# A decoder trunk on one core: high weight parts cast apart from low ones at the mixer's end, and a later place for two transposes

## The chip, the cores and the metric

The kernel runs on one core of one Trainium2 chip. The metric is device time in microseconds (us) of one execution, as the median of several runs. Five engines work side by side, each through its own list of instructions in a fixed order: PE (TensorE: matmuls and transposes), DVE (VectorE), ACT (ScalarE), POOL (GpSimd) and SP, which here only issues the copies of weights from memory (DMAs).

## The reference

The model takes 256 tokens of 1024 channels through two layers. Each layer is: half a gated FFN, a mixer, half a gated FFN, each on a normalised input and added to the residual.

```
for layer in range(2):
    h = rms_norm(x, ffn1_norm[layer])
    x = x + 0.5 * swiglu(h, gate, up, down)          # d_ff = 2816
    h = rms_norm(x, mix_norm[layer])
    if layer == 0:                                   # "mixer AB"
        proj = h @ ab_w_in                           # 1024 -> 1536
        u_pool, u_val, u_gate = split(proj)          # 512 each
        y_pool = pool_mixer(u_pool)                  # 4 windows, a 128x128 map each, a scale
        y_conv = conv_module(u_val, u_gate)          # GLU, 31 taps, LayerNorm, swish
        y = concat(y_pool, y_conv) @ ab_w_out
    else:                                            # "mixer C", sparse attention
        y = dsa_attention(...) @ c_w_out
    x = x + y
    h = rms_norm(x, ffn2_norm[layer])
    x = x + 0.5 * swiglu(h, gate, up, down)
return rms_norm(x, final_norm)
```

## The kernel before

All weights are float32 in memory. Each weight tile is split on the chip into a high part `hi` (a cast, on ACT, line 158) and a low part `lo` = raw - hi (on DVE, line 182), and a product is made of three: hi x hi, lo x hi and hi x lo. The activations are split in the same way (`hT` holds the normalised input, transposed, high and low; `kh`/`kl` are the high and low parts of a hidden tile).

Weight tiles come in one fixed `stream` and are of two kinds: `gu` (1024 input channels by 256 columns, 1 MB, cast and subtracted in two pieces) and `d` (128 rows by 1024 columns, 0.5 MB, one piece). There are three raw buffers of each kind; a raw buffer is free for the next copy when the tile's low part is made (`issue`, line 130). There are three high and three low buffers of `gu`, five of `d`. `pump(n)` makes the high and the low part of the next n tiles that have buffers, the two always together; `weights(kind)` pumps until the tile that is needed is split.

The stages are written out by hand in program order, and every engine works in that order: there is no scheduler that moves anything. The 256 tokens are two halves of 128, token tile A and token tile B. At the end of each stage `tail` (line 352) does the last four K tiles of the output product for tile A, in two column halves with accumulators `a0`, `a1`, then for tile B (`b0`, `b1`). Behind each half, `norm_half` adds the sum to the residual `x` (DVE, line 227) and squares it (ACT, line 229); `norm_apply` makes the reciprocal root (POOL, line 235) and the two scaled halves `h` (DVE, line 238). A's two halves are transposed on PE (line 245) between the K tiles of `b1`, and copied to `hT` as high (ACT, line 249) and low (DVE, line 252). B's two halves are transposed by `finish_b`, in the middle of the next stage's first matmuls.

The next stage begins in `wide` (line 292): three `gu` tiles, numbered 0, 1, 2 below. The first pass (line 304) takes A's tokens with the high parts of tiles 0 and 1, then come B's transposes, then the pass of tile 2. The second pass goes tile by tile: B's tokens with the high part (line 312), all tokens with the low part (line 315), two column halves each. From the fourth tile on the FFN goes on with `hidden` (lines 284 and 287) and `down_all` (line 341).

I call the stretch from the last K tiles of one stage to the second pass of the next a seam. The seam that the change touches is the one from mixer AB (`mixer_ab`) to the second FFN. There, before, the call of `tail` has `units` (0, 0), so nothing is pumped behind a half, and `between` 1, so one tile is pumped between the residual sums of A's first and second half: it is tile 0 of the FFN. Tiles 1 and 2 are pumped when `wide` is called. In the middle of mixer AB, `pool_map` maps two pooled groups: two matmuls into two halves of one PSUM bank, then for each half a scaled cast on ACT (line 598) and the rest on DVE (line 599).

Of the kernel before, what the change touches and what calls it, by code (L numbers as in the profile page):

```python
# [39 lines left out]
def tile_trunk(ctx: ExitStack, tc: tile.TileContext, d: dict, out: bass.AP):  # L40
# [35 lines left out]
    def f32(ap):  # L76
        return ap.bitcast(F32)
# [106 lines left out]
            issue()  # L184
        return True

    def weights(kind):
        k = state["used"]
        state["used"] += 1
        assert stream[k][0] == kind, (k, stream[k], kind)  # L190
        while order[kind].index(k) >= split[kind]:
            assert pump(1), ("no buffer", k, kind)
        return parts[k]

    def done(kind, n=1):
        spent[kind] += n
# [95 lines left out]
    def wide(items, finish_b, pumps=True, ahead=2):  # L292

        banks = []
        for n, (w, cols, _) in enumerate(items):
            if n == len(items) - 1:
                finish_b()
            bs = []
            for cs, tag in cols:
                m = cs.stop - cs.start  # L300
                b = bank(tag)
                bv = b[:m].rearrange("p (l n) -> p l n", l=2)
                for c in range(NCH):
                    pe.matmul(bv[:, :, 0:P], w[0][:, c, cs], hT[:, c, 0:2, 0:P],  # L304
                              start=c == 0, stop=False, skip_group_check=True)
                bs.append((bv, cs))
            banks.append(bs)
        pump(ahead)
        for (w, cols, use), bs in zip(items, banks):
            for bv, cs in bs:  # L310
                for c in range(NCH):
                    pe.matmul(bv[:, :, P:2 * P], w[0][:, c, cs], hT[:, c, 0:2, P:2 * P],  # L312
                              start=False, stop=False, skip_group_check=True)
                for c in range(NCH):
                    pe.matmul(bv[:, 0, :], w[1][:, c, cs], hT[:, c, 0, :],  # L315
                              start=False, stop=c == NCH - 1, skip_group_check=True)
            done("gu")
            use([bv for bv, _ in bs])
            if pumps:
                pump(1)  # L320
# [28 lines left out]
    def new_accs():  # L349
        return [[bank(ATAG[t][h]) for h in range(2)] for t in range(2)]  # L350

    def tail(accs, kts, ws, coef, g, units=(1, 1), between=0):

        n = len(kts)

        def mm(t, half, k):
            down_mm(accs[t][half], kts[k], ws[k], t, half, False, k == n - 1)

        ss = small(2)
        for half in range(2):  # L360
            for k in range(n):
                mm(0, half, k)
            pump(units[half])
            norm_half(0, half, accs[0], coef, ss)
            if half == 0:
                pump(between)
        ha = list(norm_apply(0, ss, g))
        for k in range(n):
            mm(1, 0, k)
        for k in range(n):  # L370
            mm(1, 1, k)
            if k < 2:
                transpose_half(0, k, ha, ATAG[0][k])
        done("d", n)
        ss = small(2)
        for half in range(2):
            norm_half(1, half, accs[1], coef, ss)
        hb = list(norm_apply(1, ss, g))

        def finish_b():  # L380
            for half in range(2):
                transpose_half(1, half, hb, ATAG[1][half])
        return finish_b
# [12 lines left out]
    def ffn(n, finish_b, gname, final=None, extra=None, first=None):  # L396
# [20 lines left out]
        else:  # L417
            tags = [("g0", "g1"), ("g2", "g3"), ("a0", "a1")]
            two = (slice(0, P), slice(P, 2 * P))
            wide([(weights("gu"), list(zip(two, tags[i])), use(i)) for i in range(3)], finish_b)  # L420
        g = load_gain(gname)
        accs = None
        for i in range(3, NFF):
# [74 lines left out]
    def mixer_ab(finish_b, gname):  # L498
# [90 lines left out]
        def pool_map(first, tag):  # L589
            b = bank(tag)  # L590
            outs = [b[:, q * 256:q * 256 + 256] for q in range(2)]
            for q, o in enumerate(outs):
                gi = first + q
                pe.matmul(o, pw[:, gi * P:gi * P + P], ms[gi], start=True, stop=True)
            for q, o in enumerate(outs):
                gi = first + q
                hi, lo = new_split()
                act.activation(hi, o, AF.Copy, scale=pscale[:, gi:gi + 1])
                dve.scalar_tensor_tensor(lo, o, pscale[:, gi:gi + 1], f32(hi),
                                         op0=ALU.mult, op1=ALU.subtract)  # L600
                kts.append((hi, lo))

        accs = {}
        ws = []
# [91 lines left out]
        tags = [("a0", "a1"), ("g0", "g1"), ("g2", "g3")]  # L696
        two = (slice(0, P), slice(P, 2 * P))
        preload(AF.Sigmoid)
        wide([(weights("gu"), list(zip(two, t)), use) for t in tags], finish_b, True, AHEAD)
        taps_pe(0, "b0")  # L700
        taps_out(0)
        load_pack(2)
# [12 lines left out]
        taps_out(3)  # L715
        preload(AF.Silu)
        last = weights("gu")
        b01 = bank("g0")
        p01 = b01[:, 0:256], b01[:, 256:512]
        narrow_group(p01[0], last, slice(0, P))  # L720
# [5 lines left out]
        out_mm(0, 0)  # L726
        out_mm(1, 0)
        windows(0, p01)
        variance("g2")
        out_mm(0, 1)  # L730
        pool_diff(0)
# [10 lines left out]
        out_mm(0, 3)  # L742
        out_mm(1, 3)
        accs = [accs[0], accs[1]]
        return tail(accs, kts[4:8], [weights("d") for _ in range(4)], 1.0, g, (0, 0), 1)


    def bias_rows(tag):
# [15 lines left out]
    def mixer_c(finish_b, gname):  # L764
# [11 lines left out]
        def use_kw(bvs):  # L776
            wide_sum(bvs[0], 72, kw)
            pool.dma_start(k2[64:128], kw[0:64])

        two = (slice(0, P), slice(P, 2 * P))  # L780
        wide([(weights("gu"), list(zip(two, ("g0", "g1"))), use_qi(0)),
              (weights("gu"), list(zip(two, ("g2", "g3"))), use_qi(1)),
              (weights("gu"), [(slice(0, 72), "a0")], use_kw)], finish_b)
        g = load_gain(gname)


# [376 lines left out]
```

## Time and profile before

| | |
|---|---|
| median of 3 runs | 988.77 us (988.34 to 989.34) |
| profiled execution, its own time | 987.02 us |
| its span in the profile | 985.3 us |
| PE busy | 963.4 us, 98% of the span |
| DVE busy | 658.6 us, 67% |
| ACT busy | 534.3 us, 54% |
| share of the chain that ended last | PE 92%, DVE 4%, ACT 2%, issue 2% |
| mean granted clock of PE | 0.993 of 2.4 GHz |

The span is what the profiler sees of the program; 1.7 us of the execution's own time lie around it. The chain that ended last is followed back from the last instruction, at each step to what released it. PE carries nearly all of it, so what can be saved here is the time in which PE waits or runs at its lower clock.

### The profile page before, as it was taken

The page shows a single profiled execution, that of the slowest core. Times are in us where ns is not written, and L with a number is a line of the kernel's source. Part 1 is how long each engine was busy: PE and PEld are TensorE (multiplying, and loading weights), DVE is VectorE, ACT ScalarE, POOL GpSimd, SP SyncE. Part 2 cuts the span into 40 slices and gives each one's busy share as a digit, 9 for nine tenths or more (in the row PEclk, how much of TensorE's full clock was granted, in tenths as well). Part 3 has the DMA queues.
Part 4 walks back from the last instruction along what each step waited for, and adds up shares of the span by engine and source line. Part 5 has one row for each costly group of instructions (what it writes and reads, how often), then busy time and mean ns, then how long its engine had stood idle before and what let it go on. Part 6 is the DMA issues. An engine that isn't in the chain of part 4 may idle for free.

```text
span 985.3 us, 14682 instructions
## 1 busy us (share of the span) xinstructions
PE 963.4 (98%) x5720; PEld 836.3 (85%) x5720; DVE 658.6 (67%) x1083; ACT 534.3 (54%) x959; POOL 62.3 (6%) x89
## 2 busy tenths in 40 slices
PE   7999999999979999999999999999999999999997
PEld 6888888898869888888988888888899798888885
DVE  6876666678568666666686666667888658666653
ACT  5665555565556645554565555445556556555542
POOL 3000000000000000000000000000435000000000
PEclk9999999999999999999999999999999999999999
DMA  9875555535246757655365555437444527655401
GB/s 335 305 278 186 191 190 188 187 109 181 65 148 230 264 205 244 237 194 190 111 254 192 192 192 193 162 107 279 148 137 151 210 71 253 232 189 191 155 1 43
DMA packets 38021, 182.03 MB, mean 185 GB/s; under 512 B 6416, under 2 KB 6448, under 8 KB 24768
## 3 DMA queue, kind: packets, MB, share of 16 engines
q1 hardware_dynamic: 32400, 169.92, 48.6%
q0 software_dynamic: 5264, 10.92, 3.4%
q8 instruction: 45, 0.74, 0.3%
q10 hardware_dynamic: 288, 0.27, 0.1%
q14 instruction: 24, 0.20, 0.1%
HBM read 179.92 MB, written 4.22 MB: 187 GB/s over the span
## 4 chain that ended last, share of the span: by engine, by line
PE 92%; DVE 4%; ACT 2%; issue 2%; DMA 0%; POOL 0%; SPq 0%; POOLq 0%; DVEq 0%; ACTq 0%
PE g L284 29%; PE g L287 15%; PE a L341 14%; PE b L341 13%; PE g L268 4%; PE g L312 2%; PE g L315 2%; PE g L304 2%; PE a L268 1%; DVE lo L182 1%; PE b L538 1%; PE a L312 1%; PE a L315 1%; PE b L823 1%; DVE keep L969 1%
## 5 line engine op out<-in xcount | busy, mean ns | idle before, releaser
L182 DVE TENSOR_TENSOR lo<-raw,hi 128x1024 fp32r<-128x1024 f32 (+1 forms) x319 | 380.4, 1244 | 57.8 <-ACT hi L158 57.8
L158 ACT CAST hi<-raw 128x1024 fp32r<-128x1024 f32 x320 | 314.7, 1043 | 5.4 <-DMA raw<-in_c_out 2.6
L284 PE MATMUL g<-hT,hi 128*128 128x512 f32 x1248 | 310.7, 391 | 0.8 <-DVE t L327 0.8
L284 PEld LDWEIGHTS g<-hT,hi 128*128 128x128 f32 x1248 | 228.7, 188 | 44.8 <-DVE t L327 1.0
L324 ACT COPY t<-g 128x256 f32<-128x256 f32 x174 | 63.4, 372 | 222.2 <-PE g L287 205.9
L287 PEld LDWEIGHTS g<-hT,lo 128*128 128x128 f32 x1248 | 170.3, 190 | 12.2
L287 PE MATMUL g<-hT,lo 128*128 128x256 f32 x1248 | 174.0, 282 | 0.0
L327 DVE TENSOR_TENSOR t<-g,t 128x256 f32<-128x256 f32 x174 | 71.9, 421 | 137.2 <-ACT t L324 137.0
L341 PE MATMUL a<-hi,kh 128*128 128x512 f32 x208 | 82.7, 398 | 0.0
L341 PE MATMUL b<-hi,kh 128*128 128x512 f32 x208 | 82.6, 397 | 0.0
L341 PE MATMUL a<-lo,kh 128*128 128x512 f32 x208 | 81.9, 394 | 0.0
L341 PE MATMUL b<-hi,kl 128*128 128x512 f32 x208 | 81.5, 392 | 0.0
L341 PE MATMUL b<-lo,kh 128*128 128x512 f32 x208 | 81.5, 392 | 0.0
L341 PE MATMUL a<-hi,kl 128*128 128x512 f32 x208 | 81.0, 389 | 0.0
L392 ACT CAST kh<-t 128x256 fp32r<-128x256 f32 x88 | 35.7, 406 | 57.8 <-DVE t L390 57.8
L393 DVE TENSOR_TENSOR kl<-t,kh 128x256 fp32r<-128x256 f32 x88 | 37.4, 425 | 41.5 <-ACT kh L392 41.5
L388 ACT ACTIVATE t<-t 128x256 f32<-128x256 f32 x88 | 36.9, 420 | 26.1 <-DVE t L327 26.1
L235 POOL TENSOR_TENSOR sm<-sm,mhalf 128x1 f32<-128x1 f32 x11 | 6.1, 554 | 673.2 <-DVE sm L233 673.2
L341 PEld LDWEIGHTS a<-hi,kl 128*128 128x128 f32 x208 | 39.1, 188 | 8.8
L341 PEld LDWEIGHTS b<-hi,kl 128*128 128x128 f32 x208 | 39.3, 189 | 8.3
L341 PEld LDWEIGHTS b<-hi,kh 128*128 128x128 f32 x208 | 39.4, 189 | 8.2
L341 PEld LDWEIGHTS b<-lo,kh 128*128 128x128 f32 x208 | 39.4, 189 | 7.8
(210 smaller groups left out, 949.9 us busy)
## 6 DMA issues: line engine op xcount, KB each, us to landing
raw<-in_gu SPq DMA_DIRECT2D x87, 1024.0 KB, 4.8
raw<-in_dn SPq DMA_DIRECT2D x88, 512.0 KB, 5.3
raw<-in_c_qk SPq DMA_DIRECT2D x8, 1024.0 KB, 4.9
raw<-in_ab_in SPq DMA_DIRECT2D x6, 1024.0 KB, 4.8
raw<-in_ab_out SPq DMA_DIRECT2D x8, 512.0 KB, 5.2
raw<-in_c_v SPq DMA_DIRECT2D x8, 512.0 KB, 4.3
raw<-in_c_out SPq DMA_DIRECT2D x8, 512.0 KB, 4.0
eall<-escr POOLq DMA_DIRECT2D x4, 768.0 KB, 17.3
```

Source lines behind the costliest of these rows:

```text
L158: act.copy(hi[:, c], raws[k][:, c])
L182: e.tensor_tensor(lo[:, c], raws[k][:, c], f32(hi[:, c]), op=ALU.subtract)
L268: pe.matmul(dst, wt[:, c, cols], hT[:, c, part, :], start=n == 0, stop=n == len(seq) - 1)
L284: pe.matmul(b, hi[:, c, cols], hT[:, c, 0:2, :], start=c == 0, stop=False, skip_group_check=True)
L287: pe.matmul(b[:, 0:256], lo[:, c, cols], hT[:, c, 0, :], start=False, stop=c == NCH - 1, skip_group_check=True)
L312: pe.matmul(bv[:, :, P:2 * P], w[0][:, c, cs], hT[:, c, 0:2, P:2 * P], start=False, stop=False, skip_group_check=True)
L324: act.copy(t[:m], bv[:, 1, :])
L327: dve.tensor_tensor(dst[:m], bv[:, 0, :], t[:m], op=ALU.add)
L341: pe.matmul(acc, kt[a][:, ts], w[b][:, hs], start=start and n == 0, stop=stop and n == 2)
L388: act.activation(s, gv, AF.Silu)
L392: act.copy(hi, m)
L393: dve.tensor_tensor(lo, m, f32(hi), op=ALU.subtract)
```

## The change

Three things change, and all of them move instructions in mixer AB and in the seam behind it.

1. The high parts of `gu` tiles can be cast apart from the low parts. In mixer AB, behind its last input tile, tile 0 of the next FFN is pumped whole and the high part of tile 1 is cast; behind the pooled windows, the high part of tile 2. `wide` takes tiles whose high parts are there (`ahead_of`), and its `pump(ahead)` makes the low parts of tiles 1 and 2 behind B's transposes. No tile is pumped any more between the residual sums of A's halves. In the other seams `ahead_of` finds all tiles split, and the order of instructions is the same as before.
2. `pool_map` casts both groups on ACT first, then takes both rests on DVE.
3. In this seam A's transposes stand behind the second and the third K tile of `b1` instead of the first and the second.

```
+    def highs(n):
+        for _ in range(n):
+            assert begun["gu"] - spent["gu"] < hi_bufs["gu"]
+            begin("gu")
+
+    def ahead_of(kind):
+        k = take(kind)
+        while order[kind].index(k) >= begun[kind]:
+            highs(1)
+        return k
...
+    def lows(kind, k):
         while order[kind].index(k) >= split[kind]:
             assert pump(1), ("no buffer", k, kind)
...
         pump(ahead)
-        for (w, cols, use), bs in zip(items, banks):
+        for (k, cols, use), bs in zip(items, banks):
+            lows("gu", k)
+            w = parts[k]
...
-    def tail(accs, kts, ws, coef, g, units=(1, 1), between=0):
+    def tail(accs, kts, ws, coef, g, units=(1, 1), turn=(0, 1)):
...
             norm_half(0, half, accs[0], coef, ss)
-            if half == 0:
-                pump(between)
...
             mm(1, 1, k)
-            if k < 2:
-                transpose_half(0, k, ha, ATAG[0][k])
+            if k in turn:
+                transpose_half(0, turn.index(k), ha, ATAG[0][turn.index(k)])
...
+            new = [new_split() for _ in outs]
             for q, o in enumerate(outs):
-                gi = first + q
-                hi, lo = new_split()
-                act.activation(hi, o, AF.Copy, scale=pscale[:, gi:gi + 1])
-                dve.scalar_tensor_tensor(lo, o, pscale[:, gi:gi + 1], f32(hi),
-                                         op0=ALU.mult, op1=ALU.subtract)
-                kts.append((hi, lo))
+                act.activation(new[q][0], o, AF.Copy, scale=pscale[:, first + q:first + q + 1])
+            for q, o in enumerate(outs):
+                dve.scalar_tensor_tensor(new[q][1], o, pscale[:, first + q:first + q + 1],
+                                         f32(new[q][0]), op0=ALU.mult, op1=ALU.subtract)
+            kts.extend(new)
...
         last = weights("gu")
+        pump(1)
+        highs(1)
         b01 = bank("g0")
...
         windows(0, p01)
+        highs(1)
         variance("g2")
...
-        return tail(accs, kts[4:8], [weights("d") for _ in range(4)], 1.0, g, (0, 0), 1)
+        return tail(accs, kts[4:8], [weights("d") for _ in range(4)], 1.0, g, (0, 0), (1, 2))
```

The first place is DVE in the seam, from A's first residual sum (`x_86`) and second (`x_87`) to its scaled halves `h`. Before:

```order
L227 SCALAR_TENSOR_TENSOR x_86<-a_463_2625,x_86 128x512
L182 TENSOR_TENSOR lo_2805<-raw_2106,hi_2802 128x1024 x2
L227 SCALAR_TENSOR_TENSOR x_87<-a_464_2626,x_87 128x512
L233 SCALAR_TENSOR_TENSOR sm_2825<-sm_2786 128x1
L238 SCALAR_TENSOR_TENSOR h_2829<-x_86,sm_2827,gain_2508 128x512
L238 SCALAR_TENSOR_TENSOR h_2831<-x_87,sm_2827,gain_2508 128x512
```

And now:

```order
L247 SCALAR_TENSOR_TENSOR x_86<-a_467_2636,x_86 128x512
L247 SCALAR_TENSOR_TENSOR x_87<-a_468_2637,x_87 128x512
L253 SCALAR_TENSOR_TENSOR sm_2831<-sm_2800 128x1
L258 SCALAR_TENSOR_TENSOR h_2835<-x_86,sm_2833,gain_2508 128x512
L258 SCALAR_TENSOR_TENSOR h_2837<-x_87,sm_2833,gain_2508 128x512
```

The two pieces of tile 0's low part (`lo_2805`) are gone from between the sums; on ACT the two casts of its high part are gone from between the squares.

The second place is DVE a little later, from the sums of tile B (`x_88`, `x_89`) to the low part of B's transposes (`hT` from `b`). Before:

```order
L227 SCALAR_TENSOR_TENSOR x_89<-b_466_2634,x_89 128x512
L233 SCALAR_TENSOR_TENSOR sm_2878<-sm_2871 128x1
L238 SCALAR_TENSOR_TENSOR h_2882<-x_88,sm_2880,gain_2508 128x512
L238 SCALAR_TENSOR_TENSOR h_2884<-x_89,sm_2880,gain_2508 128x512
L182 TENSOR_TENSOR lo_2889<-raw_2173,hi_2886 128x1024 x2
L182 TENSOR_TENSOR lo_2897<-raw_2239,hi_2894 128x1024 x2
L252 TENSOR_TENSOR hT<-b_539_2938,hT 128x4x128
L252 TENSOR_TENSOR hT<-b_540_2945,hT 128x4x128
```

And now:

```order
L247 SCALAR_TENSOR_TENSOR x_89<-b_470_2645,x_89 128x512
L253 SCALAR_TENSOR_TENSOR sm_2884<-sm_2877 128x1
L258 SCALAR_TENSOR_TENSOR h_2888<-x_88,sm_2886,gain_2508 128x512
L258 SCALAR_TENSOR_TENSOR h_2890<-x_89,sm_2886,gain_2508 128x512
L272 TENSOR_TENSOR hT<-b_535_2928,hT 128x4x128
L272 TENSOR_TENSOR hT<-b_536_2935,hT 128x4x128
L182 TENSOR_TENSOR lo_2960<-raw_2173,hi_2556 128x1024 x2
L182 TENSOR_TENSOR lo_2965<-raw_2239,hi_2664 128x1024 x2
```

The low parts of tiles 1 and 2 moved from ahead of `hT`'s low part to behind it; on ACT the four casts of their high parts are gone from ahead of `hT`'s high part, to the middle of the mixer.

The third place is PE in the same seam: the matmuls of `b1` (three for each K tile) and the transposes of A's halves (`ident`). Before:

```order
L341 MATMUL b_466_2634<-hi_2387,kl_2706 128x512
L245 MATMUL a_520_2848<-ident,h_2829 128x128 x4
L341 MATMUL b_466_2634<-hi_2676,kh_2710 128x512
L341 MATMUL b_466_2634<-lo_2678,kh_2710 128x512
L341 MATMUL b_466_2634<-hi_2676,kl_2711 128x512
L245 MATMUL a_521_2858<-ident,h_2831 128x128 x4
```

And now:

```order
L364 MATMUL b_470_2645<-hi_2387,kl_2720 128x512
L364 MATMUL b_470_2645<-hi_2690,kh_2724 128x512
L364 MATMUL b_470_2645<-lo_2692,kh_2724 128x512
L364 MATMUL b_470_2645<-hi_2690,kl_2725 128x512
L265 MATMUL a_522_2857<-ident,h_2835 128x128 x4
L364 MATMUL b_470_2645<-hi_2744,kh_2729 128x512
L364 MATMUL b_470_2645<-lo_2746,kh_2729 128x512
L364 MATMUL b_470_2645<-hi_2744,kl_2730 128x512
L265 MATMUL a_523_2867<-ident,h_2837 128x128 x4
```

Each group of four transposes stands three matmuls further on.

## Rows read from the trace of the kernel before

**Rows 1.** Timeline of PE at the mixer seam: start, duration (us), instruction, count, [idle before <- releaser].

```profile
269.59 0.39 PE L341 MATMUL b<-hi,kh 128*128 128x512 f32 x1
...
277.18 0.66 PE L245 MATMUL a<-ident,h 128*128 128x128 f32 x4 [4.03 <-DVE h L238]
...
281.78 2.06 PE L304 MATMUL g<-hT,hi 128*128 128x256 f32 x16
...
291.02 1.33 PE L312 MATMUL g<-hT,hi 128*128 128x256 f32 x8 [1.11 <-DVE hT L252]
```

**Rows 2.** Timeline of PE at the seam from the second FFN to the third.

```profile
464.08 0.39 PE L341 MATMUL b<-hi,kh 128*128 128x512 f32 x1
...
467.49 0.60 PE L245 MATMUL a<-ident,h 128*128 128x128 f32 x4
...
468.62 0.60 PE L245 MATMUL a<-ident,h 128*128 128x128 f32 x4
...
470.45 4.00 PE L304 MATMUL g<-hT,hi 128*128 128x256 f32 x32
474.29 1.30 PE L245 MATMUL b<-ident,h 128*128 128x128 f32 x8
475.34 2.15 PE L304 MATMUL a<-hT,hi 128*128 128x256 f32 x16
477.33 1.12 PE L312 MATMUL g<-hT,hi 128*128 128x256 f32 x8
```

**Rows 3.** PE's waits, whole span: engine line <- releaser, us in total, times, longest.

```profile
PE g L312 <- DVE hT L252: 1.1, 1, 1.1
PE g L304 <- ACT hi L158: 0.8, 2, 0.6
```

**Rows 4.** Two windows: engines' busy time (count), then PE's granted clock, DMA share, GB/s.

```profile
279.00:280.00 1.00, 1.00 (x6) 0.90 (x5) 0.18 (x1) 0.20 (x1) 0.00 (x0) 0.50 0.00 0
283.00:284.00 1.00, 0.84 (x8) 0.64 (x6) 0.16 (x1) 1.00 (x3) 0.17 (x1) 1.00 0.00 0
```

**Rows 5.** Timeline of DVE at the mixer seam.

```profile
269.32 0.69 DVE L227 SCALAR_TENSOR_TENSOR x<-a,x 128x512 f32<-128x512 f32 x1
271.74 2.36 DVE L182 TENSOR_TENSOR lo<-raw,hi 128x1024 fp32r<-128x1024 f32 x2 [1.73 <-ACT hi L158]
274.01 0.68 DVE L227 SCALAR_TENSOR_TENSOR x<-a,x 128x512 f32<-128x512 f32 x1
...
285.74 4.63 DVE L182 TENSOR_TENSOR lo<-raw,hi 128x1024 fp32r<-128x1024 f32 x4
```

**Rows 6.** Timeline of DVE at the seam from the second FFN to the third.

```profile
469.88 0.69 DVE L252 TENSOR_TENSOR hT<-a,hT 128x512 fp32r<-128x512 f32 x1 [0.44 <-ACT hT L249]
470.49 1.28 DVE L227 SCALAR_TENSOR_TENSOR x<-b,x 128x512 f32<-128x512 f32 x2
...
473.46 1.42 DVE L238 SCALAR_TENSOR_TENSOR h<-x,sm,gain 128x512 f32<-128x512 f32 x2 [0.67 <-POOL sm L235]
475.58 1.35 DVE L252 TENSOR_TENSOR hT<-b,hT 128x512 fp32r<-128x512 f32 x2 [0.71 <-ACT hT L249]
```

**Rows 7.** Timeline of ACT in the middle of the mixer.

```profile
247.92 0.47 ACT L598 ACTIVATE kh<-g,cpk 128x256 fp32r<-128x256 f32 x1 [7.55 <-PE g L594]
248.94 0.48 ACT L598 ACTIVATE kh<-g,cpk 128x256 fp32r<-128x256 f32 x1 [0.55 <-DVE kl L599]
...
253.96 1.05 ACT L158 CAST hi<-raw 128x1024 fp32r<-128x1024 f32 x1 [0.74 <-PE b L341]
```

**Rows 8.** Timeline of DVE in the middle of the mixer.

```profile
248.43 0.48 DVE L599 SCALAR_TENSOR_TENSOR kl<-g,cpk,kh 128x256 fp32r<-128x256 f32 x1 [2.31 <-ACT kh L598]
249.45 0.48 DVE L599 SCALAR_TENSOR_TENSOR kl<-g,cpk,kh 128x256 fp32r<-128x256 f32 x1 [0.55 <-ACT kh L598]
```

**Rows 9.** Timeline of SP's issues, and the raw weights' time from issue to landing.

```profile
218.16 15.93 SPq L145 DMA_DIRECT2D raw<-in_gu  x3
...
DMA to landing us min/median/max: 3.4/4.9/7.3
```

More of the change, by code (lines that the diff above doesn't have):

```diff
@@ L185, in pump, with take @@
         return True
-    def weights(kind):
+    def highs(n):
+        for _ in range(n):
+            assert begun["gu"] - spent["gu"] < hi_bufs["gu"]
+            begin("gu")
+    def take(kind):
         k = state["used"]
@@ L190, in weights @@
         assert stream[k][0] == kind, (k, stream[k], kind)
+        return k
[3 more added lines that the diff above has]
+            highs(1)
+        return k
+    def weights(kind):
+        k = take(kind)
+        lows(kind, k)
+        return parts[k]
+    def lows(kind, k):
         while order[kind].index(k) >= split[kind]:
             assert pump(1), ("no buffer", k, kind)
-        return parts[k]
     def done(kind, n=1):
@@ L298, in wide @@
             bs = []
+            w = parts[w]
             for cs, tag in cols:
@@ L419, in ffn @@
             two = (slice(0, P), slice(P, 2 * P))
-            wide([(weights("gu"), list(zip(two, tags[i])), use(i)) for i in range(3)], finish_b)
+            wide([(ahead_of("gu"), list(zip(two, tags[i])), use(i)) for i in range(3)], finish_b)
         g = load_gain(gname)
@@ L698, in mixer_ab @@
         preload(AF.Sigmoid)
-        wide([(weights("gu"), list(zip(two, t)), use) for t in tags], finish_b, True, AHEAD)
+        wide([(ahead_of("gu"), list(zip(two, t)), use) for t in tags], finish_b, True, AHEAD)
         taps_pe(0, "b0")
@@ L780, in mixer_c @@
         two = (slice(0, P), slice(P, 2 * P))
-        wide([(weights("gu"), list(zip(two, ("g0", "g1"))), use_qi(0)),
-              (weights("gu"), list(zip(two, ("g2", "g3"))), use_qi(1)),
-              (weights("gu"), [(slice(0, 72), "a0")], use_kw)], finish_b)
+        wide([(ahead_of("gu"), list(zip(two, ("g0", "g1"))), use_qi(0)),
+              (ahead_of("gu"), list(zip(two, ("g2", "g3"))), use_qi(1)),
+              (ahead_of("gu"), [(slice(0, 72), "a0")], use_kw)], finish_b)
         g = load_gain(gname)
```

## The prediction

> **What bounds the kernel now.** The page gives PE 98% of the span and nearly all of the chain that ended last, so I read the profile from PE. PE's list of waits comes first: the two waits of [rows 3], together 1.9 us, lie at the mixer seam, as does a single wait of 4.03 us for A's scaled halves [rows 1]. Then the timelines of the mixer seam [rows 1] and of the seam from the second FFN to the third [rows 2], which has the same instructions in the same order on PE and none of these waits. The reader should lay one over the other, from the first matmul of `b0` to the first matmul of the second pass (L312): 291.02 - 269.59 = 21.43 us at the mixer, 477.33 - 464.08 = 13.25 us at the FFN seam. The excess, 8.18 us, is what this seam can give.
>
> Where it lies: in the FFN seam fifteen matmuls stand between 464.08 and the transposes at 467.49, so one takes 0.2273 us. At the mixer PE is through with the same fifteen at 272.99 and the transposes begin at 277.18: 4.19 us late. From there to the first pass takes 281.78 - 277.18 = 4.60 us against 470.45 - 467.49 = 2.96: 1.64 us. The window of 279 to 280 shows why, a granted clock of 0.50, which is the lower level, 1.2 GHz; it follows PE's 4.03 us without work, and at 283 to 284 it is 1.00 again [rows 4]. Then 0.8 us of waiting for casts of high parts and 1.1 for the low part of `hT` [rows 3]. That makes 7.7; the other 0.45 I put down to the restarts.
>
> DVE shows the cause [rows 5]. A's first residual sum starts at 269.32, its second only at 274.01; between them stands tile 0's low part (2.36 us), which itself waited 1.73 us for ACT's casts. At 285.74 four more pieces (4.63 us) stand ahead of B's `hT`.
>
> **A's chain.** With no tile between the halves, the second sum follows the first at 269.32 + 0.70 = 270.02; the last matmul of `a1` is issued by then, since `b0` starts at 269.59. From second sum to first transpose took 277.18 - 274.01 = 3.17 us, so the first half could be transposed at 273.19. PE is through the first K tile of `b1` at 272.99 and through the second 3 x 0.2273 = 0.68 us later, at 273.67, which is where the transposes now stand. So PE doesn't wait for A at all, the 4.19 us go, and the lower clock with them.
>
> **B's chain, and what the later place costs.** I count from the first matmul of `b0`, at 0. A's transposes begin after 18 matmuls, at 4.09; those of the second half 468.62 - 467.49 = 1.13 later, at 5.22; the end of `b1` stays at 470.45 - 464.08 = 6.37. DVE takes A's low parts ahead of B's sums. In the FFN seam the second low part starts 469.88 - 468.62 = 1.26 behind its transposes, B's sums 0.61 after that, B's two `h` 2.97 after those and last 1.42 [rows 6]. Here: low part 6.48, sums 7.09, `h` 10.06 to 11.48. PE's first pass, 3.84 long in the FFN seam (470.45 to 474.29), ends at about 10.2 to 10.6, the upper end if it waits for A's second low part (7.17 at the end). So PE now waits for `h`: the second half's four transposes start at 11.5 and end 0.53 later (half of 475.34 - 474.29), at 12.03; the pass of tile 2 takes 477.33 - 475.34 = 1.99, so L312 starts at 14.02, say 14.05 with one handover. The FFN seam has 13.25: the later place of the transposes costs 0.8 us. If DVE got to B's sums sooner than I count, it costs nothing; more than 0.8 it can't well cost, since everything moves by one K tile, 0.68, and small waits. B's `hT` low part ends 475.58 + 1.35 - 475.34 = 1.59 behind the transposes, at 13.6, ahead of L312.
>
> **The moved casts and low parts.** Ahead of `pool_map` come four cast pieces on ACT, at 1.05 each 4.2 us [rows 7], and two low pieces on DVE, 2.36 us [rows 5]. ACT had been idle for 7.55 us there [rows 7], DVE for 2.31 [rows 8]. On ACT 3.3 us of cover are left. On DVE the low part overruns its cover by 0.05 us, but the rest now waits for both casts anyway. The raw data must be there: the third of the copies left SP at 218.16 + 15.93 - 0.33 = 233.8 and the slowest landing took 7.3 us, so all had landed by 241.1 [rows 9], when ACT has just begun. The last two pieces (tile 2) stand ahead of the cast at 253.96, which had waited 0.74 us; it moves by about 1.3 us, its low part is taken when DVE gets to it, and PE wants it only in the tail. I take nothing for all this; with no cover it would be at most the 4.2 us of ACT. On SP the copy of the fourth tile moves ahead of three copies of `d` tiles, and starts when tile 0's raw buffer comes free, some 25 us sooner than before. It delays nothing, for those `d` copies wait for their own buffers.
>
> Behind B's `hT` DVE has tiles 1 and 2 to do, 2.36 each: done at 13.6 + 2.4 = 16.0 and 18.3. PE wants the first at 14.05 + 4.8 = 18.9 (two column halves of 1.92, then 0.96 of high parts; L312 and L315 take 0.96 each in the FFN seam), the second at 22.7: 2.9 and 4.4 us of cover. The sums that follow them in the queue, and the low parts of tiles 3 and 4, come up to 5 us later than now against the second pass. PE needs tile 3 only 11.5 us after L312 begins, and a DVE that is 67% busy makes up 5 us in two or three tiles.
>
> **`pool_map`.** ACT's second cast waited 0.55 us for DVE, though DVE was reading the other half of the bank [rows 7, 8]: the engines took turns, 247.92 to 249.93 for one map. Now two casts, then two rests: one handover instead of three, and two like instructions overlap by about 0.1 (B's two sums take 1.28, one takes 0.69). Some 0.25 a map, two maps. DVE is ahead of PE by little there, so I take 0.15 us for the start of `b0`; the bounds are 0 and 0.5.
>
> **The sum.** L312 moves from 291.02 to 269.59 - 0.15 + 14.05 = 283.49, 7.5 us sooner. Behind it PE is busy with matmuls to the next seam, so nothing eats the gain. Span 985.3 - 7.5 = 977.8, the execution's own time 987.02 - 7.5 = 979.5. The profiled execution is 1.75 us below the median of the three runs, so the median is 988.77 - 7.5 = **981.3 us**. About 0.2%, 2 us, is what a measurement of this kernel can tell from no change.
>
> **The rivals.** (1) The later place costs nothing, because DVE takes B's sums sooner than I count: the seam then has the FFN's 13.25, and the gain is 8.18 + 0.15 = 8.3, so 980.5. For it: with the earlier place PE would wait only 0.2 us, so both places are near each other. Against: DVE's fixed order. Chance 0.17.
>
> (2) A new wait. The low parts of tiles 1 and 2 come late, at L315 of tile 1. It decides when they are over 2.9 us later than I count, as when B's `hT` is itself late by casts still ahead of it; then B's chain keeps its old waits and only A's goes: 4.19 + 1.64 - 0.8 = 5.0 us, 983.8. Against: both orders show nothing ahead of `hT`. Chance 0.07.
>
> (3) The clock drops all the same, in the three short waits of up to 0.9 us in sum that the seam keeps, and costs the 1.64 us again: 982.9. Against: at 283 to 284 the clock was 1.00 while PE waited 0.6 us for a cast [rows 3, 4]. Chance 0.04. The Trainium skill has this rule in "TensorE: Matmul & The Clock Gate", section "A second HAM failure mode: psum-queue depth-cycling": small idle gaps between groups of matmuls can make the clock swing between its two levels. By that rule the sum would be rival 3's; the trace so far disagrees for waits of this size.
>
> (4) Slower. ACT is held at the cast of tile 1's high part, ahead of `pool_map`, because its high buffer or its raw data isn't free; everything behind it in the mixer, and PE with it, waits. Each us past 247.9 counts in full, and it outweighs the gain from 7.5 us on, when the cast ends past 255.4. 4 us more than that would give 993. Against: landing by 241.1, and three high buffers for one tile in use. Chance 0.03.
>
> (5) No change that can be told: the seam's gain is given back in the FFN, where DVE starts with 5 us of arrears. It needs PE to wait over 5 us there, and a DVE with a third of its time free has 2.9 us of cover at the tightest place that I found. Chance 0.03.
>
> **How the numbers follow.** My forecast holds 0.66, itself from 980.5 to 982.3. Faster by over 0.2%: 0.66 + 0.17 + 0.07 + 0.04 = 0.94; within 0.2%: 0.03; slower: 0.03. The range takes in rivals 1 and 3 and the microsecond over which the runs of this kernel spread: 979.8 to 983.3.
>
> **What would show it.** No wait of PE before A's transposes, and a clock of 1.00 through the seam; `b0` to L312 in 14.0 us; in it waits of PE for `h` of B, some 0.5 us; B's sums on DVE right behind A's second low part; ACT's four casts inside the old 7.55 us of idle time; no wait for a low part in the second pass. Wrong it would be if `pool_map` came later than 247.9, if the second pass waited at L315, or if the next FFN's PE waited for `d` tiles.

## The result, and the profile after

The changed kernel takes 980.13 us in the median of 4 runs (977.87 to 980.83), the kernel before 989.06 us in 4 runs beside it. The ratio is 0.9912 with a 95% interval of 0.9899 to 0.9924, that is 7.5 to 10.0 us faster. I had said 981.3, in a range of 979.8 to 983.3. The profiled execution has a span of 978.4 us against 985.3.

The timeline of PE at the mixer seam in the changed kernel, which answers to [rows 1]:

```profile
269.76 0.39 PE L364 MATMUL b<-hi,kh 128*128 128x512 f32 x1
...
273.84 0.60 PE L265 MATMUL a<-ident,h 128*128 128x128 f32 x4
...
274.98 0.60 PE L265 MATMUL a<-ident,h 128*128 128x128 f32 x4
...
276.11 0.64 PE L325 MATMUL g<-hT,hi 128*128 128x256 f32 x4
276.98 3.61 PE L325 MATMUL g<-hT,hi 128*128 128x256 f32 x28 [0.23 <-DVE hT L272]
280.68 1.32 PE L265 MATMUL b<-ident,h 128*128 128x128 f32 x8
281.75 2.16 PE L325 MATMUL a<-hT,hi 128*128 128x256 f32 x16
283.75 1.12 PE L335 MATMUL g<-hT,hi 128*128 128x256 f32 x8
```

The wait of 4.03 us before A's transposes is gone. From the first matmul of `b0` to the second pass it takes 283.75 - 269.76 = 13.99 us, where the kernel before took 21.43. One small wait is noted in it, for A's second low part, between four matmuls of the first pass and the other 28. The wait for B's `h`, which I had put at some 0.5 us, is noted in no list, but the starts show it: from its first matmul to B's transposes the first pass takes 280.68 - 276.11 = 4.57 us, where the FFN seam took 474.29 - 470.45 = 3.84 [rows 2]. Of these 0.73 us some 0.4 stand at A's second low part (276.98 - 276.11 less four matmuls of 0.12) and some 0.3 ahead of B's transposes, and together they are nearly all that parts this seam (13.99) from that one (13.25). Three windows over the seam, with the granted clock behind the five engines' busy times, show the upper level all through, where [rows 4] had 0.50:

```profile
269.50:276.00 6.50, 6.50 (x34) 5.40 (x33) 3.41 (x6) 2.31 (x6) 0.55 (x1) 1.00 0.02 8
276.00:278.00 2.00, 1.77 (x14) 1.52 (x13) 1.77 (x3) 0.58 (x2) 0.00 (x0) 1.00 0.00 0
278.00:280.00 2.00, 2.00 (x19) 2.00 (x18) 0.41 (x3) 0.95 (x4) 0.55 (x1) 1.00 0.00 0
```

DVE's timeline shows the new order, as [rows 5] showed the old one: both sums of A in one row, B's sums right behind A's second low part, and the low parts of tiles 1 and 2 (four pieces) last.

```profile
269.36 1.28 DVE L247 SCALAR_TENSOR_TENSOR x<-a,x 128x512 f32<-128x512 f32 x2
...
276.23 0.69 DVE L272 TENSOR_TENSOR hT<-a,hT 128x512 fp32r<-128x512 f32 x1 [0.44 <-ACT hT L269]
276.84 1.28 DVE L247 SCALAR_TENSOR_TENSOR x<-b,x 128x512 f32<-128x512 f32 x2
...
279.87 1.42 DVE L258 SCALAR_TENSOR_TENSOR h<-x,sm,gain 128x512 f32<-128x512 f32 x2 [0.73 <-POOL sm L255]
281.99 1.36 DVE L272 TENSOR_TENSOR hT<-b,hT 128x512 fp32r<-128x512 f32 x2 [0.70 <-ACT hT L269]
283.26 4.62 DVE L182 TENSOR_TENSOR lo<-raw,hi 128x1024 fp32r<-128x1024 f32 x4
```

ACT's timeline in the middle of the mixer, which answers to [rows 7]: the early casts lie in the old gap of 7.55 us and leave 3.77 of it, and the two casts of a map now stand together.

```profile
240.69 3.87 ACT L158 CAST hi<-raw 128x1024 fp32r<-128x1024 f32 x4
248.33 0.84 ACT L618 ACTIVATE kh<-g,cpk 128x256 fp32r<-128x256 f32 x2 [3.77 <-PE g L615]
```

One wait is new. It lies in the second FFN, 50 us behind the seam, at the small matmul that makes the bias rows for mixer C; the first two rows are from the list of waits from 284 to 345 (who waited for whom, us in total, times, longest), the third is from PE's timeline:

```profile
ACT hi L158 <- DMA raw<-in_dn: 1.5, 1, 1.5
...
PE g L778 <- DVE t L350: 0.5, 1, 0.5
```

```profile
334.75 0.60 PE L778 MATMUL g<-t,rb 32*16 32x256 f32 x2 [0.51 <-DVE t L350]
```

### The profile page after: what moved, and what is told of

The parts are those of the page before. It is cut to its first block, busy times and chain, and to the rows that moved or that the text cites. A ratio compares the mean times of both kernels' runs of the same rounds, so it can differ in the third digit from the quotient of the medians.

```text
span 978.4 us, 14679 instructions
## 1 busy us (share of the span) xinstructions
PE 961.7 (98%) x5720; PEld 835.5 (85%) x5720; DVE 658.5 (67%) x1083; ACT 533.6 (55%) x959; POOL 62.4 (6%) x89
## 3 DMA queue, kind: packets, MB, share of 16 engines
q0 software_dynamic: 5264, 10.92, 3.4%
## 4 chain that ended last, share of the span: by engine, by line
PE 89%; DVE 6%; ACT 2%; issue 2%; DMA 1%; SPq 0%; POOL 0%; POOLq 0%; DVEq 0%; ACTq 0%
PE g L304 27%; PE g L307 14%; PE a L364 14%; PE b L364 13%; PE g L288 4%; DVE lo L182 3%; PE g L335 2%; PE g L338 2%; PE g L325 2%; PE a L288 1%; PE b L559 1%; ACT hi L158 1%; PE b L847 1%; DMA raw<-in_dn 1%; DVE keep L993 1%
```

## The experiments

Times of whole runs of one kernel spread by up to 3 us (below), so each profile is also read in three stretches between starts on PE: the seam, from the first matmul of `b0` to the second pass; the second FFN, from there to A's first transposes at its end; and mixer C, from A's transposes at the end of the third FFN to those at the end of mixer C. For the kernel before these are 291.02 - 269.59 = 21.43, 467.49 - 291.02 = 176.47 and 790.69 - 652.83 = 137.86.

| kernel | median us (runs) | ratio to before, 95% | span | seam | second FFN | mixer C |
|---|---|---|---|---|---|---|
| before | 989.06 (4) | | 985.3 | 21.43 | 176.47 | 137.86 |
| before, again | 988.65 (1) | | 986.9 | 22.11 | 176.47 | 137.89 |
| changed | 980.13 (4) | 0.9912 (0.9899, 0.9924) | 978.4 | 13.99 | 176.80 | 137.97 |
| changed, again | 979.92 (1) | | 978.1 | 13.98 | 176.94 | 136.48 |
| 1 early turn | 978.87 (4) | 0.9906 (0.9891, 0.9921) | 975.9 | 13.36 | 176.54 | 136.44 |
| 2 other bank | 978.59 (4) | 0.9903 (0.9889, 0.9916) | 976.5 | 13.98 | 176.26 | 136.47 |
| 3 both | 978.38 (4) | 0.9903 (0.9890, 0.9917) | 976.6 | 13.35 | 176.30 | 137.76 |
| 4 old map | 980.51 (5) | 0.9923 (0.9909, 0.9937) | 977.2 | 13.99 | 176.27 | 136.49 |
| 5 low part between | 981.98 (4) | 0.9933 (0.9916, 0.9949) | 980.2 | 15.60 | 176.27 | 137.98 |
| 6 casts late | 981.88 (4) | 0.9932 (0.9917, 0.9947) | 980.6 | 15.44 | 177.18 | 137.82 |
| 7 only no split | 984.82 (4) | 0.9955 (0.9940, 0.9971) | 983.1 | 18.98 | 176.27 | 137.67 |
| 8 kept busy | 984.73 (4) | 0.9960 (0.9945, 0.9975) | 983.1 | 20.28 | 176.47 | 136.49 |
| 9 busy in C | 977.32 (4) | 0.9892 (0.9875, 0.9908) | 976.5 | 13.36 | 176.26 | 136.48 |

Kernels 1 to 6 start from the changed kernel, 7 and 8 from the one before, 9 from kernel 3. Kernels 1 to 4 shared the runs of the kernel before, and so did 5 to 8, and 9 with the two repeats.

**1. The early turn.** My text held that the later place of A's transposes costs 0.8 us.

```
-        return tail(accs, kts[4:8], [weights("d") for _ in range(4)], 1.0, g, (0, 0), (1, 2))
+        return tail(accs, kts[4:8], [weights("d") for _ in range(4)], 1.0, g, (0, 0), (0, 1))
```

> The changed kernel with A's transposes back behind the first and second K tile of b1. Theory (the later place puts A's second low part, and with it B's sums on DVE, one K tile later): the seam from the first matmul of b0 to the second pass takes 13.2 to 13.4 us instead of 13.99, with a wait of PE of at most 0.2 us before A's transposes; about 0.7 us faster than the changed kernel, a ratio to the kernel before near 0.9905. Rival (the earlier place makes PE wait for A's halves, so that the place is worth its cost): a wait of 0.6 us or more before the transposes, and a seam of 14.0 us or longer.

The seam fell to 13.36, by 0.63 us. PE's timeline of this kernel has no wait noted before the transposes, which stand at 273.04, 3.40 us behind the first matmul of `b0` at 269.64; B's transposes start 10.29 behind it instead of 10.92:

```profile
273.04 0.65 PE L265 MATMUL a<-ident,h 128*128 128x128 f32 x4
274.23 0.60 PE L265 MATMUL a<-ident,h 128*128 128x128 f32 x4
...
279.93 1.32 PE L265 MATMUL b<-ident,h 128*128 128x128 f32 x8
```

So the later place loses about 0.6 us, on B's chain, and wins nothing. By medians the step can't be told.

**2. The other bank.** The bias rows are made right behind the matmuls that fill `g0` and `g1`, in `g0`; DVE must have read `g0` first.

```
-    fb = ffn(1, fb, "f1n1", extra=lambda: bias_rows("g0"))
+    fb = ffn(1, fb, "f1n1", extra=lambda: bias_rows("g2"))
```

> The changed kernel with the small matmul of the bias rows, in the second FFN, writing to bank g2 instead of g0. Theory (DVE's arrears of two low parts reach that far; the matmul waited 0.5 us because DVE was late to release g0, and cost the second FFN 0.7 us): no wait there, and the stretch from the end of the seam to the FFN's last K tiles is as short as in the kernel before: 0.6 to 0.7 us faster than the changed kernel. Rival (the 0.7 us were lost to the raw copies of d tiles or to the clock): the wait goes, but the loss stays within 0.2 us of what it was.

The wait is gone and the second FFN is 0.54 us shorter than in the first profile of the changed kernel, 0.68 than in the second. ACT's wait for a copy is still there:

```profile
ACT hi L158 <- DMA raw<-in_dn: 1.6, 1, 1.6
```

This wait goes with the loss. With the bias rows in `g0`, the matmul waited 0.2, 0.5, 0.6 and 0.9 us where ACT had waited 1.2, 1.5, 1.6 and 1.7 us for a `d` tile's copy (kernel 1, the changed kernel twice, kernel 6), and not at all where ACT had not waited (4 and 5). With `g2` PE lost nothing there, though ACT waited 1.6 us in kernel 2 and 2.2 in kernel 3. (The trace of kernel 3 puts its wait down to a matmul of PE; but the copy, issued at 311.50 and 7.8 us under way, landed at 319.3, and the cast began at 319.37.) So PE feels a late copy where its matmul needs a bank that DVE has just to read. The copy is not issued late: SP issues the two `d` copies from 28.84 us behind the start of the second pass both in the changed kernel and in kernel 4, and they took 7.1 us to land in the one and 5.7 in the other. Why, no run here shows. That the low parts which now stand behind B's transposes put DVE into arrears, and that a late copy only adds to these, is argued: no run has a copy as late without them.

**3. Both.**

> Both edits, the early place of A's transposes and the other bank for the bias rows. If the two costs are independent: 1.4 us faster than the changed kernel, a ratio to the kernel before near 0.990. Rival (the arrears of DVE only show later when the seam is shorter): no more than 0.9 us.

In the profile both savings are there, 0.64 in the seam and 0.50 in the FFN, 1.1 us in sum. The median is 1.75 us below that of the changed kernel, but the two were not run beside each other, and beside kernels 1 and 2 it differs by less than their spread. Independent, by the stretches (0.63 in kernel 1 and 0.54 in kernel 2 make 1.17), though the sum is below the 1.4 that I had said; the times don't show it.

**4. The old map.**

```
-            new = [new_split() for _ in outs]
             for q, o in enumerate(outs):
-                act.activation(new[q][0], o, AF.Copy, scale=pscale[:, first + q:first + q + 1])
-            for q, o in enumerate(outs):
-                dve.scalar_tensor_tensor(new[q][1], o, pscale[:, first + q:first + q + 1],
-                                         f32(new[q][0]), op0=ALU.mult, op1=ALU.subtract)
-            kts.extend(new)
+                gi = first + q
+                hi, lo = new_split()
+                act.activation(hi, o, AF.Copy, scale=pscale[:, gi:gi + 1])
+                dve.scalar_tensor_tensor(lo, o, pscale[:, gi:gi + 1], f32(hi),
+                                         op0=ALU.mult, op1=ALU.subtract)
+                kts.append((hi, lo))
```

> The changed kernel with the pooled map as before, cast and rest in turn for each half. Theory (one handover instead of three): the stretch from the second last input projection's end to the first matmul of b0 is 0.2 to 0.3 us longer than in the changed kernel, each map takes DVE and ACT 2.0 us instead of 1.76; total time 0.25 us longer, within the noise. Rival (the map lies beside PE's work): the maps are longer, and b0 starts as early as in the changed kernel against the projection.

From the projection's matmuls ahead of the first map to the first matmul of `b0` it takes 25.73 us, in the kernel before 25.72 and 25.75, in the changed kernel 25.48 and 25.46. ACT's timeline has the turns back:

```profile
248.86 0.48 ACT L619 ACTIVATE kh<-g,cpk 128x256 fp32r<-128x256 f32 x1 [3.77 <-PE g L615]
249.88 0.47 ACT L619 ACTIVATE kh<-g,cpk 128x256 fp32r<-128x256 f32 x1 [0.55 <-DVE kl L620]
```

So the two maps give 0.25 us, and the early casts and the early low part, which this kernel keeps, cost nothing.

**5. A low part between the sums.**

```
             norm_half(0, half, accs[0], coef, ss)
+            if half == 0:
+                pump(between)
...
-        return tail(accs, kts[4:8], [weights("d") for _ in range(4)], 1.0, g, (0, 0), (1, 2))
+        return tail(accs, kts[4:8], [weights("d") for _ in range(4)], 1.0, g, (0, 0), (1, 2), 1)
```

What is pumped there is tile 1's low part alone.

> The changed kernel with one pump between A's residual sums again; it is now tile 1's low part alone, 2.36 us on DVE, whose high part is long there, so nothing on ACT. Theory (whatever stands between the two sums on DVE delays A's chain, and PE has 0.68 us or less of cover): second sum at 2.4 us later, PE waits 1.6 to 1.8 us before A's transposes, the seam takes 15.5 to 15.9 us instead of 13.99, clock stays 1.00; 1.7 us slower than the changed kernel. Rival (only the wait for ACT's casts hurt, or the low clock): the seam stays within 0.3 us of 13.99.

DVE's timeline, and PE's behind it:

```profile
270.61 2.35 DVE L182 TENSOR_TENSOR lo<-raw,hi 128x1024 fp32r<-128x1024 f32 x2
272.87 0.69 DVE L247 SCALAR_TENSOR_TENSOR x<-a,x 128x512 f32<-128x512 f32 x1
```

```profile
276.04 0.66 PE L265 MATMUL a<-ident,h 128*128 128x128 f32 x4 [1.40 <-DVE h L258]
```

The seam is 15.60, 1.6 us longer, with the clock at 1.00. That is the price of 2.35 us on DVE between the sums, less the cover of PE. The early place of the low part is needed, not only the early cast.

**6. The casts late.** The two calls of `highs(1)` in `mixer_ab` are left out; `ahead_of` then casts tiles 1 and 2 when `wide` is called.

```
         pump(1)
-        highs(1)
...
         windows(0, p01)
-        highs(1)
```

> The changed kernel without the two early casts: tile 0 is still split in the mixer, the high parts of tiles 1 and 2 are cast when the next stage begins, ahead of B's transposes on ACT, their low parts stay behind. Theory (the early low part of tile 0 and the low parts' later place give most; the early casts save PE a short wait for tile 1 and some delay of B's high part): the seam takes 14.7 to 15.2 us, 0.7 to 1.2 us slower than the changed kernel. Rival (the early casts are what made the gain): 16 us or more. Second rival (they do nothing): 14.0.

The seam is 15.44, a little over what I had said. PE's timeline has a wait for tile 1's cast, in two pieces of which the first is shown; on ACT's, below it, the four casts stand right ahead of B's high part:

```profile
280.44 0.74 PE L325 MATMUL g<-hT,hi 128*128 128x256 f32 x4 [1.27 <-ACT hi L158]
```

```profile
279.36 3.88 ACT L158 CAST hi<-raw 128x1024 fp32r<-128x1024 f32 x4
283.56 1.08 ACT L269 CAST hT<-b 128x512 fp32r<-128x512 f32 x2 [0.32 <-PE b L265]
```

So the early casts are worth 1.45 us of the seam's 7.4; neither nothing nor most.

**7. Only no split.** In the kernel before, `between` is 0 in place of 1; nothing else is changed.

```
-        return tail(accs, kts[4:8], [weights("d") for _ in range(4)], 1.0, g, (0, 0), 1)
+        return tail(accs, kts[4:8], [weights("d") for _ in range(4)], 1.0, g, (0, 0), 0)
```

> The kernel before, with nothing pumped between A's sums and nothing else changed: all three tiles are split at the start of the next stage. Theory (A's chain is freed, but three tiles now stand ahead of B's transposed parts and PE's first pass waits for tile 0's cast): no wait before A's transposes beyond 0.2 us, clock 1.00, but PE waits 3 us and more in the first pass and for B's low part; seam 17 to 18 us, gain 3.5 to 4.5 us on the kernel before. Rival (the split between the sums was the whole cost): the full 7 us. Second rival (the tiles' time only moves): no gain.

A's transposes come 3.51 us behind the start of `b0`, so A's chain is free, but the seam is 18.98, not 17 to 18. On PE's timeline there is a wait of 2.96 us for tile 0's cast, and on DVE's all six low pieces stand ahead of B's low part:

```profile
279.90 6.70 PE L304 MATMUL g<-hT,hi 128*128 128x256 f32 x32 [2.96 <-ACT hi L158]
```

```profile
281.16 6.90 DVE L182 TENSOR_TENSOR lo<-raw,hi 128x1024 fp32r<-128x1024 f32 x6
```

The clock, which I had expected at 1.00, falls behind this wait: the granted clock is 0.50 from 279 to 285, as two windows show, and the 32 matmuls take 286.44 - 279.90 = 6.54 us instead of 3.84 [rows 2].

```profile
280.00:281.00 1.00, 1.00 (x5) 0.98 (x5) 1.00 (x2) 1.00 (x2) 0.00 (x0) 0.50 0.00 0
284.00:285.00 1.00, 1.00 (x6) 1.00 (x6) 1.00 (x2) 0.59 (x1) 0.00 (x0) 0.50 1.24 256
```

```profile
286.44 1.03 PE L245 MATMUL b<-ident,h 128*128 128x128 f32 x8
...
289.23 1.00 PE L312 MATMUL g<-hT,hi 128*128 128x256 f32 x7
```

```profile
287.98 1.28 DVE L252 TENSOR_TENSOR hT<-b,hT 128x512 fp32r<-128x512 f32 x2
```

Not all of that counts, since DVE too holds the second pass: its six low pieces end when B's low part begins, at 287.98. In both profiles of before and in kernel 8 the second pass begins 0.74 us behind that start, here 289.23 - 287.98 = 1.25. So I estimate the low clock at 0.5 us of this seam, and the seam without it at 18.5, still above what I had said, because of the six low pieces. Its time, 4.4 us below before (2.9 to 5.9), lies in what I had said; its seam and its clock don't. The theory's direction was right. Taking the split out alone brings 2.4 to 3.1 us of seam (against the two profiles of before); the other 5, the low clock here among them, need the early casts and the low parts behind.

**8. Kept busy.** In the kernel before, 18 matmuls of the identity by itself stand on PE where it waits for A's halves; their results are unused.

```
+            if k == 0 and fill:
+                fb = bank("g0")
+                for _ in range(fill):
+                    pe.matmul(fb[:, 0:P], ident, ident, start=True, stop=True)
             if k < 2:
                 transpose_half(0, k, ha, ATAG[0][k])
...
-        return tail(accs, kts[4:8], [weights("d") for _ in range(4)], 1.0, g, (0, 0), 1)
+        return tail(accs, kts[4:8], [weights("d") for _ in range(4)], 1.0, g, (0, 0), 1, 18)
```

> The kernel before with 18 idle matmuls of 128 columns (identity by identity, into a bank that is free, their result unused) put on PE where it waits for A's halves. Theory (the granted clock of 0.50 behind the wait comes from PE's 4 us without work, and costs 1.64 us): the wait shrinks to under 1 us, the clock stays 1.00, the seam takes 19.6 to 20.0 us instead of 21.43; 1.6 us faster than the kernel before. Rival (the lower clock has another cause, or costs nothing): the clock falls all the same, or the seam stays at 21.4.

PE's timeline (a matmul of these operands shows as two), and the window behind it:

```profile
273.38 4.18 PE L375 MATMUL g<-ident 128*128 128x128 f32 x36
277.57 0.66 PE L245 MATMUL a<-ident,h 128*128 128x128 f32 x4
...
280.58 2.08 PE L304 MATMUL g<-hT,hi 128*128 128x256 f32 x16
283.71 0.74 PE L304 MATMUL g<-hT,hi 128*128 128x256 f32 x4 [1.05 <-ACT hi L158]
```

```profile
278.00:280.00 2.00, 2.00 (x14) 1.69 (x12) 0.87 (x2) 1.17 (x2) 0.00 (x0) 1.00 0.34 139
```

The clock stays at 1.00, and from the transposes to the first pass it takes 280.58 - 277.57 = 3.01 us instead of 4.60: the low clock came from PE's idle time, and cost in this stretch the 1.6 us that I had read. The seam, at 20.28 a little over what I had said, gains 1.15 only, since PE then waits longer for a cast, 1.05 us where it was 0.6. The time falls by more than the 1.6 us that I had said (2.5 to 5.4): this kernel's mixer C is the short one, and that of before the long one in both profiles. The mean granted clock of all its four runs is 0.996; none of the 25 runs of before whose clock is on record is above 0.993.

**The kernel before and the changed one, again.**

> The kernel before, once more, for its second profile. Theory (mixer C has two lengths by chance: behind the same two waits of PE, 2.0 us in all, the granted clock falls to 0.50 in some executions and not in others, and costs 1.4 us): the stretch from the second to the third pair of FFN seams, 137.9 us in the first profile, is 137.7 to 138.0 again or 136.4 to 136.5, and nothing between; the mixer AB seam stays at 21.4. Rival (the profile of before was an odd one): the seam differs by more than 0.3 us.

Mixer C came out as said, the seam did not: 22.11 instead of 21.43. Two windows and PE's timeline show why: the granted clock is at 0.50 from 278 on, as soon as PE starts again, and stays there to 283, where in the first profile PE still had most of the first microsecond at the upper level:

```profile
278.00:279.00 1.00, 0.91 (x5) 0.91 (x5) 0.70 (x2) 0.00 (x0) 0.00 (x0) 0.50 1.05 442
282.00:283.00 1.00, 1.00 (x4) 0.81 (x3) 1.00 (x2) 0.00 (x0) 0.00 (x0) 0.50 0.00 0
```

```profile
278.09 1.12 PE L245 MATMUL a<-ident,h 128*128 128x128 f32 x4 [4.00 <-DVE h L238]
...
283.40 1.83 PE L304 MATMUL g<-hT,hi 128*128 128x256 f32 x14
```

From the transposes to the first pass it takes 5.31 us here, 4.60 in the first profile, 2.96 at full clock [rows 2]. The wait is the same, 4.00 us where it was 4.03; what it costs at the low clock is 1.6 us of this stretch in one execution and 2.3 in the other, and a seam more than 0.3 us off is what I had written down for the rival, that the first profile was an odd one.

> The changed kernel, once more, for its second profile. The mixer AB seam stays within 0.1 us of 13.99, mixer C is 137.7 to 138.0 or 136.4 to 136.5; the wait at the bias rows is 0.5 us where ACT waited over 1 us for a d tile's copy, and near 0 where it did not. Rival: the seam's length changes from run to run by as much as the total does.

The changed kernel's seam is 13.98 again, and its wait at the bias rows 0.6 us with 1.6 us of ACT waiting for a copy. Its mixer C is 136.48 this time, 1.5 us shorter.

**9. Busy in mixer C.** There PE waits 0.92 and 1.11 us for the first two groups of probabilities, in every kernel but the ninth, and the clock falls behind it in some executions. In the first profile of the changed kernel a window behind that wait has 0.50, and 16 matmuls take 711.71 - 708.31 = 3.40 us; in that of kernel 2, with the same waits, 1.00 and 709.90 - 707.90 = 2.00. First the changed kernel's timeline and window, then those of kernel 2:

```profile
708.31 3.60 PE L288 MATMUL g<-hT,hi 128*128 128x256 f32 x16
711.71 1.20 PE L288 MATMUL g<-hT,lo 128*128 128x256 f32 x8
```

```profile
709.00:710.00 1.00, 1.00 (x6) 1.00 (x6) 1.00 (x1) 0.24 (x1) 0.19 (x1) 0.50 0.00 0
```

```profile
707.90 2.16 PE L288 MATMUL g<-hT,hi 128*128 128x256 f32 x16
709.90 1.12 PE L288 MATMUL g<-hT,lo 128*128 128x256 f32 x8
```

```profile
709.00:710.00 1.00, 1.00 (x10) 1.00 (x10) 1.00 (x2) 0.00 (x0) 0.00 (x0) 1.00 0.00 0
```

Kernel 9 fills both waits:

```
+                if fill[hh]:
+                    fb = bank("b0")
+                    for _ in range(fill[hh]):
+                        pe.matmul(fb[:, 0:P], ident, ident, start=True, stop=True)
                 b = bank(tags[hh])
...
-                transposes(s - 2, ("a0", "a1"))
+                transposes(s - 2, ("a0", "a1"), (4, 5) if s == 2 else (0, 0))
```

> The changed kernel with both edits (early place of A's transposes, other bank for the bias rows) and nine idle matmuls of 128 columns in mixer C, four ahead of the first transposed probabilities and five between the two groups, where PE waits 0.9 and 1.1 us; their result is unused. Theory (the clock's fall there is what makes the lengths differ): mixer C takes 136.4 to 136.8 us in the profile with the clock at 1.00, the times spread less, and the median is 0.5 to 1.4 us below that of the kernel with both edits alone, near 977.5. Rival (the filling only moves the wait, or the fall has another cause): clock 0.50 there again, or a median within 0.3 us.

Its timeline of PE and a window behind the waits:

```profile
705.59 0.70 PE L928 MATMUL a<-ident,t 128*128 128x128 f32 x3
706.13 1.28 PE L924 MATMUL b<-ident 128*128 128x128 f32 x10
707.40 0.70 PE L928 MATMUL a<-ident,t 128*128 128x128 f32 x3
```

```profile
708.00:710.00 2.00, 2.00 (x19) 2.00 (x19) 2.00 (x2) 0.79 (x3) 0.75 (x1) 1.00 0.16 45
```

Mixer C takes 136.48 us with the clock at 1.00, and the median is 977.32, the lowest of all; its runs lie within 1.0 us, those of kernel 3 within 1.9, of the changed kernel within 3.0. Its ratio to the kernel before is 0.9892 (0.9875 to 0.9908), 9 to 12 us faster. Against the changed kernel it was not run side by side; its slowest run, 978.23, lies below three of that kernel's four. Kernel 3, 1.06 us slower by the median, which is in what I had said, was not run beside it either. That PE does not wait there any more is shown; that this is what keeps the clock up is argued. Five of twelve profiles without filling are just as short, and kernel 8, which fills nothing in mixer C, has four runs within 0.7 us, all at 0.996, as this one has.

## Why the prediction was right

The forecast was the likeliest case, 981.3 us, and the measured 980.13 lies in its own range. Step by step:

**What bounds the kernel, and the excess of the seam.** Right. The seam lost 7.44 us against the first profile of before, 8.13 against the second, of an excess that I had read as 8.18.

**A's chain.** Right. Transposes 4.08 us behind the first matmul of `b0` (I had 4.09), no wait, clock 1.00. Kernel 8 shows that the low clock was a consequence of the wait, and worth the 1.6 us up to the first pass; at the second pass 1.15 of them are left.

**B's chain and the later place.** Right. Second low part of A at 276.23 - 269.76 = 6.47 (6.48), B's sums at 7.08 (7.09), `h` at 10.11 (10.06), end of B's transposes at 11.99 (12.03), second pass at 13.99 (14.05). PE waited for `h`, by some 0.3 us where I had some 0.5. Kernel 1 shows the cost of the later place, 0.63 us, where I had 0.8. Rival 1, that it costs nothing, is out.

**The moved casts and low parts.** Right for the mixer: kernel 4 keeps them and needs 25.73 us to `b0`, as the kernel before. By one of my own signs the forecast would be wrong: `pool_map`'s first cast came at 248.33, later than 247.9. But it stands 4.05 us behind the projection's matmuls in both kernels (247.92 - 243.87, 248.33 - 244.28); all of the mixer began later in this execution, and the sign should have been such a distance. Wrong for the arrears behind the seam. I had said that DVE makes up 5 us in two or three tiles, with 2.9 us of cover at the tightest place that I found. There was a tighter one that I had not looked for: the matmul of the bias rows, in a bank that DVE has just to read. It cost 0.3 to 0.5 us against the kernel before, 0.5 to 0.7 against kernel 2, in the executions in which a copy of a `d` tile landed late. This is rival 5's mechanism at a tenth of its price, and my sentence that nothing eats the gain behind the seam was wrong by as much.

**`pool_map`.** Right kind, size 0.25 us where I took 0.15 of 0 to 0.5.

**The sum.** It was made against one execution, and that one was short: in the second profile of before the low clock of the same wait costs 0.7 us more. Seam, map and FFN add up to 7.44 + 0.25 - 0.33 = 7.4 for the first profiles and to 8.13 + 0.29 - 0.47 = 7.95 for the second; the timed ratio says 7.5 to 10.0. What is left of the 8.9 us between the medians, about a microsecond, I put down to stretches that the change does not touch: mixer C has two lengths, 1.4 us apart, and the end of the first FFN (A's transposes there), ahead of all that was changed, lies between 196.25 and 197.82 in the thirteen profiles. The runs' mean granted clock goes with their time. Of 25 runs of the kernel before, ten at 0.989 took 988.67 to 989.87 us, six at 0.991 took 987.41 to 988.65, and nine at 0.993, the one that I worked from among them, took 986.99 to 987.80; the changed kernel took 977.87 in its one run at 0.996 and 980.07 to 980.83 in the three at 0.994 and 0.995. In which stretch a run without a profile lost its time is not shown. I had taken a microsecond for the spread of this kernel's runs; these 25 lie within 2.9. So the seam was foreseen; that the median came as near as 1.2 us to the forecast is partly luck.

Of the other rivals, none came: no wait at L338 in the second pass (2), no fall of the clock in the seam's short wait (3), ACT not held ahead of `pool_map` (4).

## What to carry to other kernels

Lay the seam that waits over a seam of the same program that doesn't, count offsets from one common start, and go through each engine's fixed order: here that gave each step of a chain over three engines to 0.1 us. Work that only has to be done some time belongs where its engine is idle, and what is left of it behind the last instruction that another engine waits for, not ahead; but an engine that is put into arrears will be felt at the next place where somebody needs a buffer that it has just to read, even 50 us later, so look through all such places. Read a wait of PE with the clock behind it: behind the seam's 4 us the next stretch cost 1.6 to 2.3 us more at the low clock, of which 1.15 us of the 1.6 reached the seam's end.

## What the hardware showed that I had not expected

The same wait of PE has no fixed price. Behind 4.0 us at the mixer seam the clock fell in both profiles of before, but at a price of 1.6 or 2.3 us; in kernel 7 it fell behind 2.96; behind 0.92 and 1.11 us in mixer C it fell in seven of twelve profiles without filling and not in the other five, at 1.4 us a time (137.7 to 138.0 against 136.4 to 136.5), whatever the kernel. "TensorE: Matmul & The Clock Gate" of the Trainium skill, section "What's actually happening" in its first part, says that the window in which the chip judges PE's activity runs by itself, not from the kernel's start; the trace agrees, in that one and the same wait did and did not pull the clock down. With PE kept busy by unused matmuls it stayed up in both places; for the seam the four runs of kernel 8 at 0.996 bear that out, in mixer C it may have been chance.
